# The down product of a hybrid encoder block: row blocks added onto banks, columns finished in two halves, T2 and T4 on VectorE

## Chip, cores and metric

The kernel runs on one core of a Trainium2 chip. The metric is device time in microseconds (us) of one execution; the figures below are the median, lowest and highest of three runs, and one more execution was taken with the hardware profiler.

## What is computed

One layer of a bidirectional hybrid encoder on x of shape (1, 512, 1024) in float32. The change concerns the last part only, the down product of the gated convolution MLP with the norm and residual behind it.

```python
x = x + _rmsnorm(merged @ w_out, g_post_mix)          # x1
h2 = _rmsnorm(x, g_pre_ffn)
...
hid = h @ w_up                                         # 1024 -> 2 x 2816
hid = conv(hid, conv_w) + conv_b
a, b = jnp.split(hid, 2, axis=-1)
return (jax.nn.gelu(a) * b) @ w_down                   # (512, 2816) @ (2816, 1024)
...
x = x + _rmsnorm(mlp, g_post_ffn)
```

## The kernel before

Every float32 product is done as three matmuls on a high and a low part (`split`: ACT copies the high part, L75; VectorE subtracts the low part, L82). Weights lie in HBM as blocks of 128 x 1024 (`wall`), and `units` lists in which order and in which form they are wanted. `w_get` hands out the next unit and prepares those that follow, as many as five of size two with the one handed out: an SP transfer into a raw tile (four of these), then the forms, then `split` into the slots `w4` (nine of these). All engines run their own queue in order; the order within a queue is set by a scheduler that simulates the program, so it is not always that of the source.

The 22 row blocks of `w_down` (128 rows each) are used in two ways. The first 18 make 9 pairs (`DP`), and each pair is a 2 x 2 block product done by a scheme with seven products instead of eight (M1 to M7, `UNITS`). A pair needs two units per half of the output columns: form `q` (the raw quarters, 768 columns) and form `t` (T1 to T4, 1024 columns, made in `w_down`: T1 and T3 by VectorE in one instruction, L167, T2 and T4 by GpSimd, L171 and L172). The left-hand forms come from `down_forms`, of which seven are made while the up product runs (`EAGER`) and two in the first half of the down product. `products` runs nine pairs x seven products x six matmuls of 256 columns (L974) into seven PSUM banks, once for the output columns 0 to 511 and once for 512 to 1023; `combine` (L980 to L994) then forms the four quarters `c11`, `c12`, `c21`, `c22` of each half from the seven banks.

The last 4 row blocks (`RES_DOWN`) are kept aside: their weights are split into tiles that stay (`held`), the left-hand side by `two_parts` during the second half (`some`). When both halves are done, the last loop goes over the 4 row tiles of 128 rows (`NT`) and both column halves: 12 matmuls of 512 columns, two additions of the `combine` results (L1025), the square with its row sum on ACT (L802), the multiplication by `gpf` (L1029); then `row_scale` on GpSimd (L810), the final multiply and add (L1033) and the transfer out (L1036), issued by SP and ACT in turn.

Of the kernel before, what the change touches and what calls it, by code (L numbers as in the profile page):

```python
# [12 lines left out]
AF = mybir.ActivationFunctionType  # L13
ALU = mybir.AluOpType

P = 128
D = 1024
# [12 lines left out]
NBLK = 74  # L30
WARM = 18
RES_OUT = 6
RES_DOWN = 4
DOWN0 = NW - NF
DP = (NF - RES_DOWN) // 2
# [8 lines left out]
def tile_block(ctx: ExitStack, tc, xT, x, wall, par, cs, decay, wsp, bsp, gpost, gffn, out):  # L44
# [45 lines left out]
    while i < NW:  # L90
        pair = [(f, i) for f in ("B11", "B21", "T1", "T2", "T3", "T4", "B22")]
        if U0 <= i < GATE0:
            units += pair
            i += 2
        elif GATE0 <= i < GATE1:
            units += pair[:4] + [("blk", i + 2)] + pair[4:] + [("blk", i + 3)]
            i += 4
        elif DOWN0 <= i < DOWN0 + 2 * DP:
            units += [("q", i), ("t", i)]
            i += 1  # L100
        else:
            units.append(("blk", i))
            i += 1
# [5 lines left out]
    def slot(n, at=0, w=1024):  # L109
        return sb.tile([P, 1088], F32R, tag="w4", bufs=9, name=nm(n))[:, at : at + w]  # L110

    def w_block(i):
        raw = raw_tile() if i else raw0
        resident = RES0 <= i < RES1 or i >= NW - RES_DOWN
# [9 lines left out]
        else:  # L124
            hi, lo = slot("wh"), slot("wl")
# [32 lines left out]
    def w_down(form, i):  # L158
# [5 lines left out]
        else:  # L164
# [6 lines left out]
            nc.gpsimd.tensor_tensor(out=raw[:, 512:768], in0=raw[:, :256], in1=b[:, 256:512], op=ALU.add)  # L171
            nc.gpsimd.tensor_tensor(out=raw[:, 768:], in0=raw[:, 512:768], in1=b[:, 512:768], op=ALU.add)  # L172
# [120 lines left out]
    wst = const("wst", [P, S])  # L293
# [69 lines left out]
    rbc = const("rbc", [P, S])  # L363
# [593 lines left out]
    M1, M2, M3, M5, M6, M7, M4 = range(7)  # L957

    def products(between):
        m = [None] * 7  # L960
        for j in range(DP):
            between(j)
            for n, (unit, at, act) in enumerate(UNITS):
                if n in (0, 3):
                    wh, wl = w_get()
                if j == 0:
                    m[n] = ps()
                f = slice(at * 256, (at + 1) * 256)
                ah, al = dforms[j][act]
                for t in range(2):  # L970
                    c = slice(t * P, (t + 1) * P)
                    o = m[n][:, t * 256 : (t + 1) * 256]
                    for i, (a_, w_) in enumerate(((ah, wh), (ah, wl), (al, wh))):
                        nc.tensor.matmul(  # L974
                            o, a_[:, c], w_[:, f], start=j == t == i == 0, stop=j == DP - 1 and i == 2,
                            skip_group_check=True,
                        )
        return m

    def combine(m):  # L980

        e1, e5, e3, uu = tmp("e1"), tmp("e5"), tmp("e3"), tmp("uu")
        c11, c12, c21, c22 = (blk(n="c") for _ in range(4))
        copy(e1, m[M1])
        v.tensor_add(c11, m[M2], e1)  # L985
        copy(e3, m[M3])
        copy(e5, m[M5])
        v.tensor_add(uu, m[M6], e1)
        v.tensor_add(e1, m[M7], uu)  # L989
        v.tensor_add(c21, m[M4], e1)  # L990
        v.tensor_sub(c22, e5, e1)
        v.tensor_add(e3, e3, e5)  # L992
        v.tensor_sub(c12, e3, uu)
        return [[c11, c12], [c21, c22]]  # L994

    late = list(range(EAGER, DP))
    some = []

    def first_pass(j):
        if late and j % 2:  # L1000
            down_forms(late.pop(0))

    def second_pass(j):
        if j % 2 and len(some) < RES_DOWN:
            some.append(two_parts(gp[2 * DP + len(some)]))

    cc = [combine(products(first_pass))]
    m = products(second_pass)
    held = [w_get() for _ in range(RES_DOWN)]
    cc.append(combine(m))  # L1010
    gpf = bcast(gffn, "gpf")
    for t in range(NT):
        q = small("q", 2, 4)
        xt = halves("x1")
        z = []
        for n in range(2):
            nc.sync.dma_start(xt[n], x1[t][n])
            o = ps()
            c = slice(t * P, (t + 1) * P)
            for i, ((ah, al), (wh, wl)) in enumerate(zip(some, held)):  # L1020
                mm3(o, ah[:, c], al[:, c], wh[n], wl[n], i == 0, i == RES_DOWN - 1)
            z.append(tmp("z"))
            for i in range(2):
                f = slice(i * 256, (i + 1) * 256)
                v.tensor_add(z[n][:, f], o[:, f], cc[n][t // 2][i][:, (t % 2) * 256 : (t % 2 + 1) * 256])  # L1025
            mean_square(q, n, z[n])
            if n:
                sc = row_scale(q)
            v.tensor_mul(z[n], z[n], gpf[n])  # L1029
        for i, (a, b) in enumerate(((0, 512), (512, 768), (768, 1024)) if t == NT - 1 else ((0, 512), (512, 1024))):  # L1030
            f = slice(a % S, a % S + b - a)
            zt = z[a // S][:, f]
            v.scalar_tensor_tensor(  # L1033
                out=zt, in0=zt, scalar=sc, in1=xt[a // S][:, f], op0=ALU.mult, op1=ALU.add
            )
            (nc.sync, nc.scalar)[i % 2].dma_start(out[t, :, a:b], zt)  # L1036
# [34 lines left out]
def _quads(a):  # L1071

    b = a.reshape(DP, 2, P, 2, 2, 256)
    return np.stack([
        np.concatenate([b[:, 0, :, n, 0], b[:, 1, :, n, 1], b[:, 1, :, n, 0], b[:, 0, :, n, 1]], -1) for n in range(2)
    ]).reshape(2 * DP, P, 1024)
# [65 lines left out]
```

## Time and profile before

| | |
|---|---|
| median of three runs | 853.29 us (850.13 to 853.82) |
| the profiled execution | 849.69 us |
| its span, first to last instruction | 847.5 us |
| PE busy (TensorE products) | 828.0 us, 98% |
| VectorE (DVE) busy | 612.7 us, 72% |
| ScalarE (ACT) busy | 401.9 us, 47% |
| GpSimd (POOL) busy | 126.1 us, 15% |

The profile names engines PE (products), PEld (weight loads), DVE, ACT, POOL and SP (which issues transfers). A row of a timeline gives the start, the duration, the engine and line, what is written from what, and in brackets how long the engine stood idle before and for what. A PE that counts as busy is not one at its peak, since products are pipelined.

### The profile page before, as it was taken

The page shows a single profiled execution, that of the slowest core. Times are in us where ns is not written, and L with a number is a line of the kernel's source. Part 1 is how long each engine was busy: PE and PEld are TensorE (multiplying, and loading weights), DVE is VectorE, ACT ScalarE, POOL GpSimd, SP SyncE. Part 2 cuts the span into 40 slices and gives each one's busy share as a digit, 9 for nine tenths or more (in the row PEclk, how much of TensorE's full clock was granted, in tenths as well). Part 3 has the DMA queues.
Part 4 walks back from the last instruction along what each step waited for, and adds up shares of the span by engine and source line. Part 5 has one row for each costly group of instructions (what it writes and reads, how often), then busy time and mean ns, then how long its engine had stood idle before and what let it go on. Part 6 is the DMA issues. An engine that isn't in the chain of part 4 may idle for free. (4 is left out here: it accounts for less than half of the span.)

```text
span 847.5 us, 12239 instructions
## 1 busy us (share of the span) xinstructions
PE 828.0 (98%) x4768; PEld 727.7 (86%) x4768; DVE 612.7 (72%) x966; ACT 401.9 (47%) x647; POOL 126.1 (15%) x123
## 2 busy tenths in 40 slices
PE   8999999999999999999999999999999999998993
PEld 6888888888999999999988998888888888998982
DVE  5598888877996677777755677666666555877675
ACT  6645446545664544344544564444444333443332
POOL 0010000111221111122212200000000001463601
PEclk9999999999999999999999999999999999999997
DMA  8732222213233233323556133333222221223352
GB/s 276 250 113 100 77 73 75 74 51 100 87 101 100 100 100 100 100 100 100 175 178 244 50 100 100 100 100 99 100 93 90 94 73 50 75 101 100 102 203 94
DMA packets 29242, 93.18 MB, mean 110 GB/s; under 512 B 3392, under 2 KB 4032, under 8 KB 29184
## 3 DMA queue, kind: packets, MB, share of 16 engines
q1 hardware_dynamic: 26928, 86.85, 30.6%
q0 software_dynamic: 1392, 4.46, 1.6%
q10 hardware_dynamic: 864, 1.09, 0.4%
q8 instruction: 37, 0.61, 0.3%
q14 instruction: 21, 0.17, 0.1%
HBM read 88.19 MB, written 4.19 MB: 109 GB/s over the span
## 5 line engine op out<-in xcount | busy, mean ns | idle before, releaser
L82 DVE TENSOR_TENSOR wl<-raw,wh 128x1024 fp32r<-128x1024 f32 (+1 forms) x113 | 128.5, 1147 | 105.3 <-PE ps L199 63.8
L200 PE MATMUL ps<-h2h,wl 128*128 128x512 f32 (+1 forms) x384 | 142.3, 371 | 0.0
L199 PE MATMUL ps<-h2l,wh 128*128 128x512 f32 (+1 forms) x384 | 142.2, 371 | 0.0
L198 PE MATMUL ps<-h2h,wh 128*128 128x512 f32 (+1 forms) x384 | 142.2, 372 | 0.0
L75 ACT ACTIVATE wh<-raw 128x1024 fp32r<-128x1024 f32 (+2 forms) x115 | 110.2, 970 | 43.8 <-DMA raw<-wall 24.6
L75 ACT ACTIVATE wf<-raw 128x512 fp32r<-128x512 f32 x84 | 50.8, 627 | 73.6 <-issue 30.2
L198 PEld LDWEIGHTS ps<-h2h,wh 128*128 128x128 f32 x384 | 72.1, 188 | 12.8 <-ACT h2h L858 0.3
L199 PEld LDWEIGHTS ps<-h2l,wh 128*128 128x128 f32 x384 | 72.2, 188 | 12.6
L200 PEld LDWEIGHTS ps<-h2h,wl 128*128 128x128 f32 x384 | 72.2, 188 | 12.3
L82 DVE TENSOR_TENSOR wf<-raw,wf 128x512 fp32r<-128x512 f32 x84 | 65.6, 797 | 20.0 <-ACT wf L75 19.6
L901 ACT ACTIVATE cv<-ps,part 128x512 f32<-128x512 f32 x44 | 34.4, 781 | 87.9 <-PE ps L200 87.9
L459 PE MATMUL ps<-wh,xh 128*128 128x512 f32 x192 | 75.0, 391 | 0.0
L460 PE MATMUL ps<-wl,xh 128*128 128x512 f32 x192 | 74.9, 390 | 0.0
L461 PE MATMUL ps<-wh,xl 128*128 128x512 f32 x192 | 74.8, 390 | 0.0
L646 PE MATMUL ps<-sh,wf 128*128 128x256 f32 x384 | 72.6, 280 | 0.0
L171 POOL TENSOR_TENSOR raw<-raw,raw 128x256 f32<-128x256 f32 x18 | 25.2, 1401 | 271.1 <-DVE raw L167 253.8
L974 PE MATMUL ps<-dh,fh 128*128 128x256 f32 x216 | 60.6, 281 | 1.3 <-DVE c L985 1.3
L974 PE MATMUL ps<-dl,fh 128*128 128x256 f32 x216 | 60.5, 280 | 1.1 <-DVE dl L82 1.1
L646 PEld LDWEIGHTS ps<-sh,wf 128*128 128x128 f32 x384 | 60.8, 188 | 0.5 <-ACT u L75 0.2
L974 PE MATMUL ps<-dh,fl 128*128 128x256 f32 x216 | 60.4, 280 | 0.0
L646 PE MATMUL ps<-xh,wf 128*128 128x256 f32 x288 | 54.6, 281 | 0.0
L646 PE MATMUL ps<-sl,wf 128*128 128x256 f32 x192 | 53.6, 279 | 0.0
(276 smaller groups left out, 1873.9 us busy)
## 6 DMA issues: line engine op xcount, KB each, us to landing
raw<-wall SPq DMA_DIRECT2D x145, 512.0 KB, 3.3
x<-x SPq DMA_DIRECT2D x24, 256.0 KB, 5.7
xT<-xT SPq DMA_DIRECT2D x8, 256.0 KB, 5.5
x<-x POOLq DMA_DIRECT2D x8, 256.0 KB, 2.3
xT<-xT POOLq DMA_DIRECT2D x4, 256.0 KB, 3.8
out<-z SPq DMA_DIRECT2D x4, 256.0 KB, 2.0
out<-z ACTq DMA_DIRECT2D x3, 256.0 KB, 2.1
cs<-cs SPq DMA_DIRECT2D x2, 256.0 KB, 5.0
```

What stands on the lines that cost most here:

```text
L75: nc.scalar.activation(out=o, in_=i, func=AF.Copy)
L82: nc.vector.tensor_sub(lo, src, as32(hi))
L171: nc.gpsimd.tensor_tensor(out=raw[:, 512:768], in0=raw[:, :256], in1=b[:, 256:512], op=ALU.add)
L198: nc.tensor.matmul(o, ah, bh, start=start, stop=False)
L199: nc.tensor.matmul(o, ah, bl, start=False, stop=False)
L200: nc.tensor.matmul(o, al, bh, start=False, stop=stop)
L459: nc.tensor.matmul(acc[t], xh[k][:, c], wh[:, f], start=k == 0, stop=False)
L460: nc.tensor.matmul(acc[t], xh[k][:, c], wl[:, f], start=False, stop=False)
L461: nc.tensor.matmul(acc[t], xl[k][:, c], wh[:, f], start=False, stop=k == KD - 1)
L646: nc.tensor.matmul(o, w_[:, c], a_, start=first and k == n == 0, stop=k == 3 and n == 2, skip_group_check=True,)
L901: nc.scalar.activation(out=c, in_=o, func=AF.Identity, scale=col(CW + 3 * m + 1), bias=col(CB + m))
L974: nc.tensor.matmul(o, a_[:, c], w_[:, f], start=j == t == i == 0, stop=j == DP - 1 and i == 2, skip_group_check=True,)
```

## The change

- The 4 last row blocks are no longer a product of their own. A new function `add_whole` adds them straight onto banks of the pair products: for the row tiles 0 and 1 onto M2 and M3 (from which the quarters `c11` and `c12` follow), for 2 and 3 onto M4 (`c21`) and onto an eighth bank M8, which is added to `c22`. Its matmuls have 256 columns. A weight block now holds two row blocks for one half of the columns.
- In the first half of the columns these blocks come after the pairs 3 and 5; in the second half after all nine pairs.
- The sums of the banks run inside the last pair, right after the product that closes each bank (`steps`). In the second half the last sum is taken for each row tile in the last loop.
- The first 512 columns are finished mid-way: their share of the square sum (in two pieces, added to the other half's later) and the product with `gpf` are made after the pairs 2 to 5 of the second half (`first_share`). The last loop has only the other 512 columns.
- `two_parts` of the four left-hand blocks moves into pairs 0 to 3 of the first half.
- T2 and T4 of form `t` are made by VectorE instead of GpSimd.
- `rbc` and `wst` lie in the common pool `blk`, which has 76 tiles instead of 74. The resident tiles of the four blocks are gone; their units use the slots `w4`.

The core of the diff (removed lines of the last part and the host's reordering of `w_down` are left out):

```diff
@@ -27,12 +27,12 @@
 NW = 146
 U0, GATE0, GATE1 = 32, 40, 72
 LOOK = 4
-NBLK = 74
+NBLK = 76
 WARM = 18
 RES_OUT = 6
-RES_DOWN = 4
 DOWN0 = NW - NF
-DP = (NF - RES_DOWN) // 2
+DP = 9
+WHOLE = NF - 2 * DP
 EAGER = 7
 PRE, FFNG, LNG, LNB = 0, 8, 16, 24
@@ -95,9 +95,13 @@
         elif GATE0 <= i < GATE1:
             units += pair[:4] + [("blk", i + 2)] + pair[4:] + [("blk", i + 3)]
             i += 4
-        elif DOWN0 <= i < DOWN0 + 2 * DP:
-            units += [("q", i), ("t", i)]
-            i += 1
+        elif i == DOWN0:
+            for _ in range(2):
+                pairs = [[("q", i + j), ("t", i + j)] for j in range(DP)]
+                whole = [[("blk", i + DP)], [("blk", i + DP + 1)]]
+                for u in pairs[:4] + whole[:1] + pairs[4:6] + whole[1:] + pairs[6:] if i == DOWN0 else pairs + whole:
+                    units += u
+                i += DP + WHOLE // 2
         else:
             units.append(("blk", i))
             i += 1
@@ -111,7 +115,7 @@
     def w_block(i):
         raw = raw_tile() if i else raw0
-        resident = RES0 <= i < RES1 or i >= NW - RES_DOWN
+        resident = RES0 <= i < RES1
         if i > 0:
             nc.sync.dma_start(raw, wall[i])
         if resident:
@@ -122,7 +126,8 @@
                 hi.append(h_)
                 lo.append(l_)
         else:
-            hi, lo = slot("wh"), slot("wl")
+            at = 48 if i >= DOWN0 else 0
+            hi, lo = slot("wh", at), slot("wl", at)
             if i == 0:
                 pieces = [slice(0, P), slice(P, S), slice(S, 2 * S)]
                 for f in pieces:
@@ -168,8 +173,8 @@
                 out=raw[:, :512].rearrange(two, n=2), in0=b[:, :512].rearrange(two, n=2),
                 in1=b[:, None, 768:].to_broadcast([P, 2, 256]), op=ALU.add,
             )
-            nc.gpsimd.tensor_tensor(out=raw[:, 512:768], in0=raw[:, :256], in1=b[:, 256:512], op=ALU.add)
-            nc.gpsimd.tensor_tensor(out=raw[:, 768:], in0=raw[:, 512:768], in1=b[:, 512:768], op=ALU.add)
+            nc.vector.tensor_add(raw[:, 512:768], raw[:, :256], b[:, 256:512])
+            nc.vector.tensor_add(raw[:, 768:], raw[:, 512:768], b[:, 512:768])
         w = 768 if form == "q" else 1024
         hi, lo = slot("dh", 48, w), slot("dl", 48, w)
         split(hi, lo, raw)
@@ -290,7 +295,7 @@
     make_identity(nc, ident)
     ones = const("ones", [P, P])
     nc.gpsimd.memset(ones, 1.0)
-    wst = const("wst", [P, S])
+    wst = blk(n="wst")
     nhalf = const("nhalf", [P, 16])
     nc.gpsimd.memset(nhalf, -0.5)
@@ -360,7 +365,7 @@
             start=True,
             stop=True,
         )
-    rbc = const("rbc", [P, S])
+    rbc = blk(n="rbc")
     copy(rbc, rb)
     copy(wst[:, 0:1], rbc[:, 0:1])
     cosr, sinr = halves("cs")
@@ -954,86 +959,132 @@
     UNITS = (("q", 0, "A11"), ("q", 2, "A12"), ("q", 1, "S4"), ("t", 0, "S1"), ("t", 2, "S2"), ("t", 1, "S3"), ("t", 3, "A22"))
...
+    M1, M2, M3, M5, M6, M7, M4, M8 = range(8)
+    whole = []
+    def products(m, j, steps={}):
+        for n, (unit, at, act) in enumerate(UNITS):
+            if n in (0, 3):
+                wh, wl = w_get()
+            if j == 0:
+                m[n] = ps()
+            f = slice(at * 256, (at + 1) * 256)
+            ah, al = dforms[j][act]
+            for t in range(2):
+                c = slice(t * P, (t + 1) * P)
+                o = m[n][:, t * 256 : (t + 1) * 256]
+                for i, (a_, w_) in enumerate(((ah, wh), (ah, wl), (al, wh))):
+                    nc.tensor.matmul(
+                        o, a_[:, c], w_[:, f], start=j == t == i == 0,
+                        stop=j == DP - 1 and i == 2 and n not in (M2, M3, M4), skip_group_check=True,
+                    )
+            steps.get(n, lambda: None)()
+    def add_whole(m, t, g, w, last=False):
+        wh, wl = w
+        c = slice(t * P, (t + 1) * P)
+        for n, b in enumerate(((M2, M3), (M4, M8))[t // 2]):
+            o = m[b][:, (t % 2) * 256 : (t % 2 + 1) * 256]
+            for k in range(2):
+                f = slice(k * S + n * 256, k * S + (n + 1) * 256)
+                ah, al = whole[2 * g + k]
+                for i, (a_, w_) in enumerate(((ah, wh), (ah, wl), (al, wh))):
+                    nc.tensor.matmul(
+                        o, a_[:, c], w_[:, f], start=b == M8 and t == 2 and g == k == i == 0,
+                        stop=last and k == 1 and i == 2, skip_group_check=True,
+                    )
+    m = {}
+    m[M8] = ps()
+    late = list(range(EAGER, DP))
+    c11, c12, c21, c22 = c4 = [blk(n="c") for _ in range(4)]
+    e1, e3, uu, yy = tmp("e1"), tmp("e3"), tmp("uu"), tmp("yy")
+    def after6():
         v.tensor_add(uu, m[M6], e1)
+        v.tensor_sub(c12, m[M5], uu)
+        v.tensor_add(c12, c12, e3)
+    def after7():
         v.tensor_add(e1, m[M7], uu)
...
+        v.tensor_sub(yy, m[M5], e1)
+        v.tensor_add(c22, c22, yy)
+    steps = {
+        M1: lambda: copy(e1, m[M1]),
+        M2: lambda: v.tensor_add(c11, m[M2], e1),
+        M3: lambda: copy(e3, m[M3]),
+        M6: after6, M7: after7,
+        M4: lambda: v.tensor_add(c21, m[M4], e1),
+    }
+    for j in range(DP):
+        if j < WHOLE:
+            whole.append(two_parts(gp[2 * DP + j]))
+        if j % 2 and late:
             down_forms(late.pop(0))
...
+        products(m, j, steps if j == DP - 1 else {})
+        if j in (3, 5):
+            w = w_get()
+            for t in range(NT):
+                add_whole(m, t, j // 2 - 1, w, j == 5)
+            if j == 5:
+                copy(c22, m[M8])
     gpf = bcast(gffn, "gpf")
+    qn = [small("q", 4, 4) for _ in range(NT)]
+    zg = []
+    def first_share(t):
+        zg.append(blk(n="zg"))
+        for i in range(2):
+            src = c4[2 * (t // 2) + i][:, (t % 2) * 256 : (t % 2 + 1) * 256]
+            j = tmp("junk")
+            nc.scalar.activation(out=j[:, :256], in_=src, func=AF.Square, scale=D ** -0.5, accum_out=qn[t][:, 2 + i : 3 + i])
+            v.tensor_mul(zg[t][:, i * 256 : (i + 1) * 256], src, gpf[0][:, i * 256 : (i + 1) * 256])
+        v.tensor_add(qn[t][:, 0:1], qn[t][:, 2:3], qn[t][:, 3:4])
+    m = {}
+    e1, uu, xx, yy = tmp("e1"), tmp("uu"), tmp("xx"), tmp("yy")
+    def after6():
+        v.tensor_add(uu, m[M6], e1)
+        v.tensor_sub(xx, m[M5], uu)
+    def after7():
+        v.tensor_add(uu, m[M7], uu)
+        v.tensor_sub(yy, m[M5], uu)
+    steps = {M1: lambda: copy(e1, m[M1]), M6: after6, M7: after7}
+    for j in range(DP):
+        products(m, j, steps if j == DP - 1 else {})
+        if 1 < j < 2 + NT:
+            first_share(j - 2)
+    ww = [w_get(), w_get()]
+    m[M8] = ps()
     for t in range(NT):
...
         xt = halves("x1")
...
         for n in range(2):
             nc.sync.dma_start(xt[n], x1[t][n])
...
+        for g in range(2):
+            add_whole(m, t, g, ww[g], g == 1)
+        z, zs_ = tmp("z"), tmp("zs")
+        for i, (b, e) in enumerate((((M2, e1), (M3, xx)), ((M4, uu), (M8, yy)))[t // 2]):
+            f = slice((t % 2) * 256, (t % 2 + 1) * 256)
+            v.tensor_add(z[:, i * 256 : (i + 1) * 256], m[b][:, f], e[:, f])
+        mean_square(qn[t], 1, z)
+        v.tensor_mul(zs_, z, gpf[1])
+        sc = row_scale(qn[t])
+        zt = (zg[t], zs_)
         for i, (a, b) in enumerate(((0, 512), (512, 768), (768, 1024)) if t == NT - 1 else ((0, 512), (512, 1024))):
             f = slice(a % S, a % S + b - a)
...
+            o = zt[a // S][:, f]
             v.scalar_tensor_tensor(
...
+                out=o, in0=o, scalar=sc, in1=xt[a // S][:, f], op0=ALU.mult, op1=ALU.add
             )
...
+            (nc.sync, nc.scalar)[i % 2].dma_start(out[t, :, a:b], o)
 def _parts(a, n, w):
```

More of the change, by code (lines that the diff above doesn't have):

```diff
@@ L956, in tile_block @@
     UNITS = (("q", 0, "A11"), ("q", 2, "A12"), ("q", 1, "S4"), ("t", 0, "S1"), ("t", 2, "S2"), ("t", 1, "S3"), ("t", 3, "A22"))
[L957 to L978, printed above, removed]
@@ L994, in combine @@
[L994 to L1000, printed above, removed]
-            down_forms(late.pop(0))
[L1003 to L1010, printed above, removed]
-    gpf = bcast(gffn, "gpf")
+        v.tensor_sub(yy, m[M5], e1)
@@ L1071, in _quads, with _down @@
 def _quads(a):
[L1073 to L1076, printed above, removed]
+    b = a.reshape(DP, 2, P, 2, 256)
+    return np.concatenate([b[:, 0, :, 0], b[:, 1, :, 1], b[:, 1, :, 0], b[:, 0, :, 1]], -1)
+def _down(a):
+    r = 2 * DP * P
+    return np.concatenate([
+        p for n in range(2) for c in [a[:, n * S : (n + 1) * S]]
+        for p in (_quads(c[:r]), c[r:].reshape(WHOLE // 2, 2, P, S).transpose(0, 2, 1, 3).reshape(-1, P, 1024))
+    ])
 def _cols(a):
```

31 lines of the change are left out of this document (1 added, 30 removed).

## The prediction

> **What bounds the kernel now.** I read the page's first lines, then the stretch that the change rewrites by windows, then PE's waits, the chain of waits and the timeline of each engine there.
>
> ```profile
> span 847.5 us, 12239 instructions
> ```
>
> ```profile
> core 0: us, PE busy (x) PEld busy (x) DVE busy (x) ACT busy (x) POOL busy (x), PEclk, DMA share, GB/s
> 719.10:764.90 45.80, 45.80 (x390) 45.80 (x389) 35.52 (x44) 22.08 (x29) 23.69 (x16) 1.00 0.27 93
> 764.90:812.30 47.40, 43.56 (x370) 42.70 (x369) 33.36 (x39) 18.77 (x26) 20.47 (x16) 1.00 0.40 126
> 812.30:834.30 22.00, 21.93 (x98) 17.82 (x96) 16.95 (x34) 6.42 (x16) 1.88 (x2) 1.00 0.36 137
> 834.30:847.50 13.20, 0.00 (x0) 0.00 (x0) 6.75 (x15) 2.17 (x6) 1.86 (x2) 0.58 0.22 80
> ```
>
> ```profile
> PE ps L974 <- DVE dl L82: 2.6, 3, 1.1
> PE ps L974 <- DVE c L985: 1.3, 1, 1.3
> ```
>
> The four windows are my cut of the down product: the pairs of the first 512 columns, those of the second (with the start of the row blocks' last preparation), the four row blocks, and what comes after PE's last product. PE never pauses in the first window, loses 47.40 - 43.56 = 3.8 us in the second, works through the third, and has nothing to do in the last 13.2. So the stage can give at most the 3.8 us of pauses and part of the 13.2; the products themselves stay. The two rows of waits name the pauses: 1.3 us for a PSUM bank that `combine` had not yet read (L985), 2.6 us in three waits for the low half of a weight (L82).
>
> **Products.** Before, 756 matmuls of 256 columns and 96 of 512; after, `add_whole` makes the 96 into 192 of 256, half of them after pairs 3 and 5 of the first half, half at the end. The count of columns is the same. PE runs the 256-wide ones at two paces. The first two rows below are the start of a pair's M2 and of the next pair's M1, 36 matmuls apart; the next two are the same places in the second half.
>
> ```profile
> 759.38 0.28 PE L974 MATMUL ps<-dh,fh 128*128 128x256 f32 x1
> ...
> 763.62 0.28 PE L974 MATMUL ps<-dh,fa 128*128 128x256 f32 x1
> ...
> 775.58 0.28 PE L974 MATMUL ps<-dh,fh 128*128 128x256 f32 x1
> ...
> 779.66 0.28 PE L974 MATMUL ps<-dh,fa 128*128 128x256 f32 x1
> ```
>
> 4.24 / 36 = 0.1178 us against 4.08 / 36 = 0.1133, with a granted clock of 1.00 in both windows. The row blocks' 512-wide ones follow each other at 22.0 / 96 = 0.229, twice 0.1146. All 948 cost 107.4 us at the fast pace and 111.4 at the first window's 45.80 / 390 = 0.1174. Which pace holds seems to be decided anew after a pause; I can't say which it will be and take the middle, 0.1155, so 109.5 us.
>
> The row says that halving a matmul costs between nothing and 192 x 0.0041 = 0.8 us here. The Trainium skill, page "TensorE: Matmul & The Clock Gate", section "Back-to-back issue gap", speaks mildly against the change: it gives 262 cycles for 256 columns and 518 for 512, so two halves cost 6 cycles more than one whole. By its figures, as an estimate, the 96 halved products would add 0.24 us, which lies within the row's two ends.
>
> **Weights: the loop that takes the place of GpSimd.** The chain of waits over the second half shows one turn per pair:
>
> ```profile
> 790.00 3.42 DMA raw<-wall
> ...
> 793.52 0.06 DVE raw L167
> ...
> 794.13 0.96 DVE dl L82
> ...
> 795.15 4.84 DMA raw<-wall
> ```
>
> A weight lands, VectorE adds T1 and T3 (L167), then subtracts the low half of the pair before (L82, 768 wide); that frees a raw tile, and only then does SP start the next transfer. VectorE works in order, so L167, which waits for the transfer, stands ahead of the subtraction that allows the next one. A turn is 795.15 - 790.00 = 5.15 us, against 42 x 0.1174 = 4.93 for a pair on PE. The loader is slightly slower than PE, and where a transfer takes 4.84 instead of 3.42 PE pauses. T2 and T4 are off this loop now, since GpSimd forms them:
>
> ```profile
> L171 POOL TENSOR_TENSOR raw<-raw,raw 128x256 f32<-128x256 f32 x15 | 23.0, 1534 | 46.9 <-DVE raw L167 29.5 <-ACT dh L75 11.4 <-ACT fh L75 4.5
> L172 POOL TENSOR_TENSOR raw<-raw,raw 128x256 f32<-128x256 f32 x15 | 20.1, 1338 | 1.2
> ```
>
> ```profile
> 730.08 5.02 POOL L171 TENSOR_TENSOR raw<-raw,raw 128x256 f32<-128x256 f32 x1 [6.17 <-ACT dh L75]
> 735.18 0.73 POOL L172 TENSOR_TENSOR raw<-raw,raw 128x256 f32<-128x256 f32 x1
> ```
>
> ```profile
> 724.39 0.41 DVE L82 TENSOR_TENSOR fa<-gp,fa 128x256 fp32r<-128x256 f32 x1
> 724.73 0.41 DVE L930 TENSOR_TENSOR fs<-gp,gp 128x256 f32<-128x256 f32 x1
> ```
>
> On GpSimd they take 1.53 + 1.34 = 2.9 us a pair, once 5.02 for an addition that took 0.73 the next time. On VectorE 256-wide steps follow each other at 0.34 (724.39 to 724.73), so 0.68 a pair. The form T thus comes 2.2 us earlier, but VectorE pays 0.68, and if both additions follow L167 at once, which is what their order in the code suggests, the turn grows to about 5.8 us.
>
> Load is not the limit. First half: VectorE's 35.5 us plus 18 x 0.34 = 6.1 plus the four `two_parts` (512 wide, no more than two 256-wide steps, 0.82) come to 45 of 45.8 + 10.9 = 56.7 us. So the four and the two late `down_forms` in pairs 0 to 3 are hidden; without the row blocks behind pair 3 they would not all be. Latency is the limit: at 5.8 a turn against 42 x 0.1155 = 4.85 a pair, nine pairs lose 8.5 us. In the first half the two row blocks pay for it, each 5.5 us of PE time for one unit to load. In the second half only the lead does: five units may be loaded or in work, two pairs, of which about one, 5 us, can be used up. That leaves 3.5 us of pauses (ends: 0, if the scheduler puts the additions elsewhere, and 8.5), about what there is now.
>
> **After PE's last product.** The end of the third row tile and the last one, from the timeline:
>
> ```profile
> 836.60 1.42 DVE L1033 SCALAR_TENSOR_TENSOR z<-z,qr,x 128x512 f32<-128x512 f32 x2 [0.44 <-POOL qr L810]
> ...
> 837.93 1.08 DVE L1025 TENSOR_TENSOR z<-ps,c 128x256 f32<-128x256 f32 x3
> 838.04 0.34 ACTq L1036 DMA_DIRECT2D out<-z  x1
> ...
> 840.08 0.42 DVE L1025 TENSOR_TENSOR z<-ps,c 128x256 f32<-128x256 f32 x1
> ...
> 841.34 0.16 DVE L807 SCALAR_TENSOR_TENSOR qs<-q 128x1 f32<-128x1 f32 x1 [0.85 <-ACT junk L802]
> 841.42 0.69 DVE L1029 TENSOR_TENSOR z<-z,gpf 128x512 f32<-128x512 f32 x1
> 841.58 0.93 POOL L810 TENSOR_TENSOR qr<-qs,nhalf 128x1 f32<-128x1 f32 x1 [5.02 <-DVE qs L807]
> 842.54 1.54 DVE L1033 SCALAR_TENSOR_TENSOR z<-z,qr,x 128x512 f32<-128x512 f32 x3 [0.44 <-POOL qr L810]
> ```
>
> PE is done by 834.3 (the last window shows none of it), but the last tile's sums begin at 837.93: VectorE stands behind the tile before. Its last step ends at 842.54 + 1.54 = 844.1, 9.8 us behind PE, and 3.4 us of output follow. After the change a tile has one half row left: two 256-wide adds, one square, one multiplication, the scale and the two final steps. From the last add (840.08) to the end it took 4.0 us; with one more add ahead, 0.34, a tile's chain is 4.3. VectorE's own part is 0.68 + 0.69 + 0.16 + 1.42 = 2.95. PE gives a tile every 24 x 0.1155 = 2.8, the first 8.3 us before its end. If tile after tile runs in order, as now, VectorE ends 4 x 4.3 - 8.3 = 8.9 us behind PE; if the next tile's adds fill the waits, 3 x 2.95 + 4.3 - 8.3 = 4.9. ACT's queue decides too: the output that ACT issues (838.04) stands ahead of the next tile's square and waits for the last step. Products now come faster than the chain, which favours filling; I take the middle, 6.9, so 2.9 us gained. The first 512 columns' share (squares, multiplications) lies beside pairs 2 to 5, 4 x (2 x 0.34 + 0.16) = 3.4 us of VectorE, inside that window's 14 us of idle VectorE. The sums L985 to L993 end within the last pair and M4 instead of after PE.
>
> **The bank wait.** The 1.3 us go: `products` now calls the sums as soon as each bank closes (`steps`), and M1 of the second half gets the bank of M8, which is copied to `c22` already after pair 5. What is late next is the bank of M5, which `yy` reads only after M7; M6 of the second half may need it. Between lie M7, M4 and four products of the second half, 36 x 0.1155 = 4.2 us after M6 closes; VectorE needs five 512-wide steps up to `yy`, 5 x 0.69 = 3.5. It just fits; if a wait of L167 for its transfer falls into it, it costs up to the old 1.3.
>
> Waits that the change adds: at the end of each half VectorE's sums wait for their bank to close while the next weights' forms queue behind them, at most one product, 0.7 us, each; the lead covers it. The first share's multiplications wait for `gpf`, whose two transfers on GpSimd's queue are issued at the change of halves, two pairs (9.7 us) ahead of the first use; that queue holds no additions any more. The `x1` loads stay on SP's queue behind the last weights. All three at nothing; without the cover each stands in the pauses' upper end. The two tiles moved to the common pool (`rbc`, `wst`) and its two more buffers keep the room as it was: nothing.
>
> **Sum.** 719.1 + 109.5 (products) + 3.5 (pauses) + 6.9 + 3.4 = 842.4 us of span, 5.1 less than 847.5. The profiled execution took 849.69 us, 2.2 more than its span and 0.4% under the median of the runs shown, 853.29; I take the 5.1 off the median: 848.2 us.
>
> **Rivals.** *The loop binds in both halves* (slower): T2 and T4 ahead of the subtraction, and the lead never builds up, because pairs 0 to 3 carry `down_forms` and `two_parts`. Then 18 x 0.95 = 17.1 us less about 1 at each row block, so 15 of pauses instead of 3.5: 859.7. For it: L167 stands ahead of the subtraction today. Against it: no pause in the first window though VectorE is busy there from the start. It cancels the gain at 8.6 us of pauses, and is slower by over 0.5% from 12.9. Chance 0.14.
> *The gain goes into order* (no change): slow pace throughout (111.4), 6 us of pauses, VectorE strictly tile by tile (8.9): 848.8 of span, 854.6. It needs only that the scheduler keeps today's order. Chance 0.25.
> *All fits* (large gain): 0.5 us of pauses because the T form no longer waits for GpSimd, and a filled tail of 4.9: 837.4 of span, 843.2. Chance 0.18.
> *The change doesn't do what it says*: M5's bank is held and the middle wait stays at 1.3; that moves the forecast to 849.5 and is inside it.
>
> **How the numbers follow.** The forecast has 0.43. About 0.5%, 4.3 us, is what a measurement of this kernel can tell from no change. Forecast and large gain make faster 0.61, the second rival same 0.25, the first slower 0.14. All good ends at once give 840.6 and all bad ones (111.4, 8.5, 8.9) 857.1; I leave out the outermost and the slower rival: 842 to 856.5.
>
> **What would show it.** Right: no wait for a bank at the change of halves; GpSimd with only the scales left; VectorE's last step 5 to 9 us behind PE; pauses only in the late pairs of the second half, each for `dl`, with a turn near 5.8 between transfers. Wrong: pauses of more than 8.6 us on L82, above all in the first half, or VectorE further than 9 us behind PE.

## The result and the profile after

The changed kernel takes 841.86 us (median of four runs, 841.50 to 844.99) against 853.56 (850.13 to 855.06) for the kernel before, run beside it: a ratio of 0.9877, with a 95% interval of 0.9839 to 0.9915. So it is faster, by 1.2%. The forecast was 848.2; the median lies 6.3 us below it and 0.1 us below the low end of the stated range. A second comparison of the same two kernels (e5_new_again, below) gave 0.9893, interval 0.9868 to 0.9918.

The first lines of the page of after, and the down product in windows of its own (the pairs up to the second row block; the rest of the pairs; the row blocks of the last loop; what follows PE's last product):

```profile
span 839.8 us, 12386 instructions
PE 827.2 (98%) x4864; PEld 731.3 (87%) x4864; DVE 615.1 (73%) x996; ACT 401.5 (48%) x649; POOL 76.0 (9%) x87
```

```profile
core 0: us, PE busy (x) PEld busy (x) DVE busy (x) ACT busy (x) POOL busy (x), PEclk, DMA share, GB/s
719.30:760.40 41.10, 41.10 (x350) 41.09 (x349) 34.25 (x55) 19.84 (x27) 0.59 (x1) 1.00 0.34 109
760.40:818.40 58.00, 58.00 (x506) 57.86 (x505) 45.43 (x72) 26.37 (x42) 0.54 (x1) 1.00 0.41 133
818.40:831.40 13.00, 11.89 (x98) 11.26 (x96) 9.54 (x21) 2.17 (x6) 1.66 (x3) 1.00 0.22 83
831.40:839.80 8.40, 0.00 (x0) 0.00 (x0) 4.11 (x8) 0.72 (x2) 0.55 (x1) 0.71 0.33 125
```

PE never pauses in the pairs of either half: 41.10 of 41.10 and 58.00 of 58.00. Before, the second half lost 3.8 us. The stretch without PE at the end is 8.4 us long instead of 13.2. GpSimd, 23.69 and 20.47 us busy in the two halves before, has one step in each of the first two windows, the issue of a transfer of `gpf`, and the scale steps in the last two. All of PE's waits from 715 us on are in one line of the list of waits:

```profile
PE ps L993 <- DVE z L1076: 1.0, 2, 0.5
```

Because the down product does not begin at the same time in every execution (718.2 to 726.2 us over the traces; they differ mostly in the program's first 50 us, far ahead of the change, where PE waits 0.3 to 3.7 us for the first weights), I compare it from its own first product. "Lag" is the time from the end of PE's last product to the end of VectorE's last step, "drain" the time from there to the span's end; "stage" is the sum. The last column names PE's waits in the stage.

| kernel | PE | lag | drain | stage | PE's waits (us) |
|---|---|---|---|---|---|
| before | 115.1 | 9.9 | 3.4 | 128.4 | low halves 2.6, bank 1.3 |
| before, once more (e11_old_again) | 115.2 | 9.7 | 3.4 | 128.3 | low halves 2.4, bank 1.2 |
| after | 112.0 | 5.2 | 3.4 | 120.5 | last loop 1.0 |
| after, once more (e5_new_again) | 112.8 | 5.1 | 3.4 | 121.3 | last loop 1.1, banks 0.5 |

The stage is 7.9 us shorter, 3.2 in PE's part and 4.7 in the lag. The two profiled executions differ by about the same (849.69 and 841.63 us), the medians by 11.7.

### The profile page after: what moved, and what is told of

Read it like the earlier page. It is cut to its first block, busy times and chain, and to the rows that moved or that the text cites. A ratio compares the mean times of both kernels' runs of the same rounds, so it can differ in the third digit from the quotient of the medians.

```text
span 839.8 us, 12386 instructions
## 1 busy us (share of the span) xinstructions
PE 827.2 (98%) x4864; PEld 731.3 (87%) x4864; DVE 615.1 (73%) x996; ACT 401.5 (48%) x649; POOL 76.0 (9%) x87
## 4 chain that ended last, share of the span: by engine, by line
PE 96%; DVE 1%; DMA 1%; issue 1%; ACT 0%; POOL 0%; DVEq 0%; SPq 0%; POOLq 0%; ACTq 0%
PE ps L204 16%; PE ps L203 16%; PE ps L205 16%; PE ps L651 14%; PE ps L977 10%; PE ps L465 5%; PE ps L464 5%; PE ps L466 5%; PE ps L798 2%; PE ps L796 2%; PE ps L797 2%; PE ps L993 2%; PE ps L721 1%; DMA raw<-wall 1%; PE ps L264 1%
## 5 line engine op out<-in xcount | busy, mean ns | idle before, releaser
L82 DVE TENSOR_TENSOR wl<-raw,wh 128x1024 fp32r<-128x1024 f32 (+1 forms) x109 | 128.2, 1184 | 100.0 <-PE ps L204 63.7
L75 ACT ACTIVATE wf<-raw 128x512 fp32r<-128x512 f32 x84 | 50.8, 627 | 73.5 <-issue 30.2
L82 DVE TENSOR_TENSOR wf<-raw,wf 128x512 fp32r<-128x512 f32 x84 | 65.8, 799 | 19.9 <-ACT wf L75 19.6
L82 DVE TENSOR_TENSOR dl<-raw,dh 128x768 fp32r<-128x768 f32 (+1 forms) x36 | 39.2, 1091 | 18.7 <-PE ps L204 7.9
```

The lines of the kernel that those rows point to most:

```text
L75: nc.scalar.activation(out=o, in_=i, func=AF.Copy)
L82: nc.vector.tensor_sub(lo, src, as32(hi))
```

## The experiments

The theory after the first comparison of the traces: before, T2 and T4 on GpSimd kept ACT waiting, ACT's copies of later weights stood behind, and the weights came late; VectorE's faster additions cure that. The rivals: the row blocks in the first half give the loader slack (and the additions don't matter), or the shorter last loop alone brings the gain. Each ratio is to the kernel before, run on the same chip, over five rounds, with its 95% interval.

### e1_new_gpsimd_t and e2_old_vector_t: the two parts apart

e1 is after with T2 and T4 back on GpSimd; e2 is before with them on VectorE.

```diff
-            nc.vector.tensor_add(raw[:, 512:768], raw[:, :256], b[:, 256:512])
-            nc.vector.tensor_add(raw[:, 768:], raw[:, 512:768], b[:, 512:768])
+            nc.gpsimd.tensor_tensor(out=raw[:, 512:768], in0=raw[:, :256], in1=b[:, 256:512], op=ALU.add)
+            nc.gpsimd.tensor_tensor(out=raw[:, 768:], in0=raw[:, 512:768], in1=b[:, 512:768], op=ALU.add)
```

> The changed kernel with T2 and T4 back on GpSimd, nothing else. Theory GpSimd (its slow additions hold the T form and the ACT queue behind it, and that made the pauses before): 2 to 4 us of pauses of PE on L82 come back in the pairs, span about 842 to 844. Theory queue (the pauses came from VectorE standing at L172 for a transfer while only four raw tiles exist; the row blocks in the middle cure it): pauses stay under 0.5 us and the span stays within 1 us of 839.8.

> The kernel before with T2 and T4 on VectorE, nothing else. Theory GpSimd: the 2.6 us of waits on L82 go, only the 1.3 for the bank stays, and the span falls by about 2.5 us from 847.5. Theory queue: turns of 5.1 us between transfers remain and so do 2 to 4 us of pauses; span within 1.5 us of 847.5. My blind prediction's term (turns of 5.8 us) would give pauses of 6 us or more and a longer span.

Measured: e1 844.69 us, ratio 0.9896 (0.9876 to 0.9916), stage 120.9 (PE 112.2, lag 5.0, drain 3.7). e2 844.14 us, ratio 0.9889 (0.9870 to 0.9908), stage 120.5 (PE 111.0, lag 6.1, drain 3.4). Each part of the change alone brings as much as the whole, as far as these intervals and traces can tell; together they bring no more. The theory of the queue foresaw e1, but neither foresaw so much of e2. The windows of e2:

```profile
720.40:764.90 44.50, 44.50 (x379) 44.46 (x379) 40.78 (x65) 22.82 (x30) 0.00 (x0) 1.00 0.29 98
764.90:809.30 44.40, 44.40 (x379) 44.40 (x379) 35.85 (x55) 21.18 (x29) 1.13 (x2) 1.00 0.49 158
809.30:831.40 22.10, 22.10 (x99) 18.02 (x98) 15.73 (x33) 4.34 (x12) 2.29 (x3) 1.00 0.22 83
831.40:840.90 9.50, 0.01 (x1) 0.00 (x0) 4.36 (x11) 1.45 (x4) 0.86 (x1) 0.77 0.29 110
```

No pause is left, and the tail is short although its code is that of before. Why, the timeline of VectorE shows: first before, then e2, the first sum of the second half's banks (L985), and the first sum of the last loop (L1025).

```profile
814.62 0.68 DVE L985 TENSOR_TENSOR c<-ps,e 128x512 f32<-128x512 f32 x1
...
819.39 0.75 DVE L1025 TENSOR_TENSOR z<-ps,c 128x256 f32<-128x256 f32 x2
```

```profile
807.72 0.68 DVE L985 TENSOR_TENSOR c<-ps,e 128x512 f32<-128x512 f32 x1
...
812.49 0.75 DVE L1025 TENSOR_TENSOR z<-ps,c 128x256 f32<-128x256 f32 x2
...
835.96 1.54 DVE L1033 SCALAR_TENSOR_TENSOR z<-z,qr,x 128x512 f32<-128x512 f32 x3 [0.44 <-POOL qr L810]
```

Before, the row blocks of PE began at 812.3 and L985 ran at 814.62, 2.3 us after; in e2 they began at 809.5 and L985 ran at 807.72, 1.8 us ahead. From the first L1025 to the end of the last L1033 VectorE needs the same in both: 844.1 - 819.4 = 24.7 us and 837.5 - 812.5 = 25.0. So late weights cost twice before: 3.8 us of pauses, and a tail that started late. The chain of waits of before shows how the second cost arises:

```profile
808.09 4.57 DMA raw<-wall
812.74 1.15 ACT wh L75 x2
813.89 1.47 ACT e L75 x3
```

The last weights land at 812.7; ACT copies their high parts first, and only then the banks (`e`) that the sums start from.

Where the weights lost time shows in ACT's waits in the pairs, first before, then after, then e1:

```profile
ACT dh L75 <- POOL raw L172: 35.3, 12, 6.5
```

```profile
ACT dh L75 <- PE ps L977: 24.0, 17, 2.0
ACT dh L75 <- DVE raw L177: 7.8, 3, 3.0
```

```profile
ACT dh L75 <- POOL raw L177: 22.0, 7, 5.8
```

ACT stood 35.3 us, up to 6.5 at a time, for T4 of GpSimd, and everything else in its queue stood behind that. In after it stands mostly for PE, that is for a slot whose weights PE still reads: the loader is ahead (before, these waits came to 1.5 us). Waiting for GpSimd is not a price by itself, though. In e1 ACT still stands 22.0 us for T4, up to 5.8 at a time, and PE's only wait in the pairs is 0.3 us for a bank. With GpSimd's additions e2 also takes away the late T form and the slower subtractions of VectorE (last section); which of these counts was not taken apart.

### e12_new_gpsimd_blocks_end: does the slack do it in e1?

e1, and the row blocks of the first half behind its nine pairs, with the sums of that half behind them.

```diff
-                for u in pairs[:4] + whole[:1] + pairs[4:6] + whole[1:] + pairs[6:] if i == DOWN0 else pairs + whole:
+                for u in pairs + whole:
...
-        if j in (3, 5):
...
+    w2 = [w_get(), w_get()]
+    for t in range(NT):
+        for g in range(2):
+            add_whole(m, t, g, w2[g], g == 1)
```

> The changed kernel with T2 and T4 on GpSimd, as in e1_new_gpsimd_t, and with the row blocks of the first half behind its nine pairs instead of behind pairs 3 and 5 (the sums of M2, M3, M4 and M8 follow them). Theory slack (row blocks in the midst of the pairs give the loader time, and that is what spared e1 the pauses): 2 to 5 us of pauses on L82 or on the sums come back in the pairs of the first half, stretch 123 to 126 instead of 120.9. Rival (early two_parts and the sums at each bank's end spared them): stretch 120.5 to 122.

Measured: 844.29 us, ratio 0.9915 (0.9885 to 0.9945), stage 121.9 (PE 112.9, lag 5.0, drain 4.0).

```profile
PE ps L993 <- DVE z L1078: 1.0, 2, 0.6
PE ps L977 <- DVE dl L82: 1.0, 2, 0.6
```

The waits for low halves come back, but only 1.0 us of them. The slack of the two row blocks can so be only part of why e1 does without VectorE's additions; this run also moves the sums of the banks, and the rest wasn't taken apart.

### e4_old_five_raw and e6_old_parts_early: other cures for the old kernel

e4 gives before a fifth raw tile; e6 makes `two_parts` of the last row blocks in the first half, as after does. Both keep T2 and T4 on GpSimd.

```diff
-NBLK = 74
+NBLK = 72
...
-        return sb.tile([P, 1024], F32, tag="raw", bufs=4, name=nm("raw"))
+        return sb.tile([P, 1024], F32, tag="raw", bufs=5, name=nm("raw"))
```

```diff
     def first_pass(j):
+        if j < RES_DOWN:
+            some.append(two_parts(gp[2 * DP + j]))
...
     def second_pass(j):
-        if j % 2 and len(some) < RES_DOWN:
-            some.append(two_parts(gp[2 * DP + len(some)]))
+        pass
```

> The kernel before with five raw tiles instead of four, and 72 instead of 74 tiles in the common pool to make room. Theory queue: a transfer no longer waits for the subtraction behind L167, PE's pauses in the pairs fall from 3.9 us to under 1, span about 844 (unless the smaller pool costs something ahead of the down product, which the start of the first pair, 719.1, shows). Theory GpSimd: pauses stay at 2 to 4 us.

> The kernel before with the four two_parts moved from the second half into pairs 0 to 3 of the first, as the change does, and nothing else; T2 and T4 stay on GpSimd. Theory ACT queue (the copies of two_parts stand on ACT behind the copy of form T, which waits for GpSimd, and VectorE's subtractions wait for those copies; that is what made the weights late in the second half): the wait at the fourth pair goes, at most 1.5 us of pauses stay, the stretch falls from 128.4 to 122 to 125. Rival (the turn between transfers alone makes them late): pauses of 3 to 4 us stay, stretch 127 to 129.

Measured: e4 849.93 us, ratio 0.9953 (0.9936 to 0.9970), stage 124.4; e6 849.02 us, ratio 0.9962 (0.9944 to 0.9979), stage 126.9. PE's waits in e4, then in e6:

```profile
PE ps L974 <- DVE dl L82: 3.0, 2, 1.9
```

```profile
PE ps L974 <- DVE c L985: 4.4, 1, 4.4
PE ps L974 <- DVE dl L82: 0.6, 1, 0.6
```

With a fifth raw tile the bank wait goes and the lag falls to 6.8, half the gain, but the low halves stay late: the ring of raw tiles is not the cause alone. With `two_parts` out of the second half the low halves come nearly in time (0.6 us), although ACT still stands 30.2 us for GpSimd, and the bank wait grows to 4.4. So the waits that e6 was to cure went, and the gain that was expected of it (122 to 125) did not come. VectorE's timeline in e6 shows why:

```profile
768.26 0.69 DVE L167 TENSOR_TENSOR raw<-raw 128x512 f32<-128x512 f32 x1 [3.56 <-DMA raw<-wall]
768.87 0.68 DVE L985 TENSOR_TENSOR c<-ps,e 128x512 f32<-128x512 f32 x1
```

The sum that frees the bank stands behind an L167 that waits 3.56 us for its transfer. This is the same in-order queue that makes the turn, at another place: a wait for a transfer ahead of a step that somebody needs. The long wait costs a second time: in the 3.6 us behind it the granted clock was 0.53, and 17 products took 0.21 us each instead of 0.11, 1.7 us more.

### e3_new_share_late: what finishing the first columns mid-way is worth

After, with `first_share` taken out of the pairs and put into the last loop. A small step on each quarter, which adds zero times a result of the second half, keeps the scheduler from taking the share ahead again.

```diff
-        if 1 < j < 2 + NT:
-            first_share(j - 2)
+    for c in c4:
+        v.scalar_tensor_tensor(
+            out=c[:, 0:1], in0=yy[:, 0:1], scalar=0.0, in1=c[:, 0:1], op0=ALU.mult, op1=ALU.add
+        )
...
     for t in range(NT):
+        first_share(t)
```

> The changed kernel with the first 512 columns' squares and multiplications made behind the last pair instead of beside pairs 2 to 5 (four one-column steps tie them to the last sum). Theory: the tail is VectorE's work per row tile, so 4 x (2 x 0.34 + 0.16) + 4 x 0.16 = 4 us of VectorE more after the last pair, VectorE's last step 8 to 9 us behind PE instead of 5.2, span 842.5 to 844. Rival (the tail is a chain of waits and the added steps fill them): span within 1 us of 839.8.

Measured: 848.63 us, ratio 0.9943 (0.9923 to 0.9963), against 0.9896 for e1 in the same rounds and 0.9893 for e5 in others; stage 122.9. So mid-way finishing is worth about 2 us in the stage (122.9 - 121.3 = 1.6 and 122.9 - 120.5 = 2.4), the small tying steps included. The place is another than I thought: the lag is shorter (3.75), and PE waits instead:

```profile
PE ps L993 <- DVE z L1079: 3.4, 1, 3.4
```

VectorE, late with the shares, is late with the sum that reads the first half of a bank, and PE's next product writes to the other half of it. Behind this wait, too, the granted clock was 0.50 (835.6 to 838.5 us), and 16 gaps between products were 0.213 us instead of 0.113: 1.6 us of what e3 loses is this slowing.

### e7_new_order and e9_new_tail: the last loop

In e7 the row tiles of the last loop come in the order 0, 2, 1, 3, so that two tiles that share banks don't follow each other. e9 does that, takes `z` and `zs` from the common pool, and writes the final steps of a tile behind the sums of the next.

```diff
-    for t in range(NT):
+    for t in (0, 2, 1, 3):
```

```diff
+    for t in ORDER:
...
-        z, zs_ = tmp("z"), tmp("zs")
+        z, zs_ = blk(n="z"), blk(n="zs")
...
         v.tensor_mul(zs_, z, gpf[1])
+        if ready:
+            finish(*ready)
+        ready = (t, (zg[t], zs_), xts[t], row_scale(qn[t]))
+    finish(*ready)
```

> The changed kernel with the row tiles of the last loop in the order 0, 2, 1, 3, so that two tiles that follow each other use different banks. Theory (PE's two waits of 0.5 us in the last loop are for the other half of a bank that VectorE still reads): both waits go, PE ends 1 us earlier; VectorE's tail is its own work, so the span gains 0 to 1 us. Rival (the waits have another cause): they stay.

> The changed kernel with its last loop rearranged: row tiles in the order 0, 2, 1, 3, the two half-row tiles z and zs in the common pool instead of the six-tile ring (in run e7_new_order a square on ACT waited 5.1 us for an output that still read its tile), and the final multiply-add of a row tile written behind the next tile's sums. Theory (VectorE's tail is the serial chain add, square, scale, multiply-add of each tile, about 3.6 us a tile, and some of it can overlap): PE's two waits go (1.0 us), VectorE's last step 4 to 5 us behind PE, stretch from the first product of the pairs 118 to 119.5 instead of 120.5 to 121.3. Rival (the scheduler puts the steps back in today's order): stretch 120 to 121.

Measured: e7 846.11 us, ratio 0.9912 (0.9885 to 0.9939), stage 123.0 (PE 110.6, lag 9.0); e9 845.53 us, ratio 0.9888 (0.9857 to 0.9919), stage 119.9 (PE 110.1, lag 6.4). In e7 PE's waits for `z` are gone, and the tail is worse; ACT's timeline says where:

```profile
830.91 0.63 ACT L807 ACTIVATE junk<-z 128x512 f32<-128x512 f32 x1 [5.12 <-DMA out<-zs]
```

The square waited 5.12 us because its scratch tile, in a ring of six, was still being read by an output transfer. e9 takes that ring out of the way: PE has no wait in the whole stage, and its stage is the shortest of all. Its ratio can't be told from that of after (0.9877 and 0.9893), so it isn't shown to be better; the lag of 4 to 5 us that was expected did not come.

### e8_new_pause and e10_new_extra: the pace of the products

Apart from the slow products just named, the 256-wide products run at one of two paces in all traces. e8 adds one product near the start of the down product that waits for a copy on ACT; e10 adds the same product without anything to wait for. It goes into a bank that the first row block starts anew.

```diff
+            if j == n == 0 and whole_open:
+                d = blk(F32R, "pause")
+                copy(d[:, :P], m[M1][:, :P])
+                nc.tensor.matmul(m[M8][:, :P], d[:, :P], wh[:, :P], start=True, stop=True, skip_group_check=True)
```

```diff
+            if j == n == 0 and extra:
+                nc.tensor.matmul(m[M8][:, :P], ah[:, :P], wh[:, :P], start=True, stop=True, skip_group_check=True)
```

> The changed kernel with one deliberate pause of PE behind the first product of the first pair: ACT copies 128 columns of that bank, and an extra 128-column product with the copy (into the bank M8, which is opened later) has to wait for it, about 1 us. In the traces the 256-wide products run at 0.118 or 0.113 us apart and change over only where PE has just paused. Theory pace (a pause resets the pace to the faster one): from there on 0.1133, about 0.0043 x 500 = 2 us less for the pairs, 1 us net. Rival (the pace has another cause): 0.118 in the first half as before, about 1 us more.

> The changed kernel with one extra product of 128 columns behind the first product of the first pair, into the bank M8, which is opened later; nothing waits. In e8_new_pause, with a wait of 1.6 us at this place, all 256-wide products ran at 0.113 us. Theory pause (the wait set the pace): without it 0.118 in the first half, stretch 120.5 to 121.5. Rival (the odd product set the pace): 0.113 from there on, about 2 us less for the products, stretch 118.5 to 120.5, as far as no sum is then waited for.

Measured: e8 845.14 us, ratio 0.9910 (0.9878 to 0.9941), stage 122.5; e10 844.72 us, ratio 0.9887 (0.9852 to 0.9921), stage 122.4. The start of M2 in the second pair and of M1 in the third, 36 products apart, in e8 and in e10:

```profile
726.82 0.28 PE L977 MATMUL ps<-dh,fh 128*128 128x256 f32 x1
...
730.90 0.28 PE L977 MATMUL ps<-dh,fa 128*128 128x256 f32 x1
```

```profile
726.28 0.28 PE L977 MATMUL ps<-dh,fh 128*128 128x256 f32 x1
...
730.52 0.28 PE L977 MATMUL ps<-dh,fa 128*128 128x256 f32 x1
```

4.08 / 36 = 0.1133 us after a wait, 4.24 / 36 = 0.1178 without one, and each kernel keeps its pace from there through both halves (after itself turns from the slow to the fast one near 780 us, at the change of halves). So the wait changed the pace here, and the extra product did not, by one trace of each. A wait does not always bring the faster pace: before, 36 products from 775.58 on took 4.08 us, and 36 from 783.39 on, just behind a wait of 1.07 us, took 4.24. It didn't pay: e8 spent 1.6 us on the wait itself, and the faster PE then met a bank that VectorE had not yet read:

```profile
PE ps L977 <- DVE e L1017: 1.7, 1, 1.7
PE ps L985 <- ACT pause L75: 1.6, 1, 1.6
```

### e5_new_again and e11_old_again: the two kernels once more

Unchanged kernels, for the size of the effect and for the spread between traces.

> The changed kernel once more, unchanged, beside the other three. In the earlier traces the stretch from the first product of the down pairs to the end was 128.4 us before, 120.5 with the whole change, 120.9 with all of it but GpSimd forming T2 and T4, and 120.5 with T2 and T4 on VectorE in the old kernel and nothing else. Theory either (one cure for the late weights suffices, the parts don't add up): 120.5 +- 1 again and a ratio to the kernel before of about 0.988, the same as those two. Rival (the parts add up, the two earlier timings were held back by the state of that chip): ratio under 0.985.

> The kernel before once more, unchanged, for a second trace. Its first trace began the pairs at 719.1 us; the traces of the other kernels began them between 718.2 and 726.2, according to how long PE had waited for the very first weights. Theory: the stretch from the first product of the pairs to the end is 127.5 to 129.5 again, with 3 to 5 us of pauses of PE on L82 and L985. Rival (the pauses of the first trace were those of one execution): stretch under 126.

Measured: e5 843.87 us, ratio 0.9893 (0.9868 to 0.9918); e11, one execution, 850.59 us. Their stages stand in the first table: two traces of one kernel agree within 0.8 us there.

## Why the prediction was right, and where its size was wrong

The direction and the places were right, the size was short: 5.1 us of span forecast, 7.7 measured. The mechanism was right only in part: the prediction took T2 and T4 on VectorE for a step that lengthens the turn and keeps the pauses, and e2 shows that this step alone brings as much as the whole change. Term by term:

| term of the sum | forecast | measured in after |
|---|---|---|
| start of the stage | 719.1 | 719.3 |
| 948 products | 109.5 (107.4 to 111.4) | 112.0 - 1.0 = 111.0 |
| pauses | 3.5 (0 to 8.5) | 1.0, none of them in the pairs |
| tail lag | 6.9 (4.9 to 8.9) | 5.2 |
| drain | 3.4 | 3.4 |

**The turn: the step that failed.** I put T2 and T4 right behind L167, ahead of the subtraction, and got a turn of 5.8 us. VectorE's timeline of after, one turn (L172 is now the line of T1 and T3, L176 and L177 are T2 and T4):

```profile
767.06 0.69 DVE L172 TENSOR_TENSOR raw<-raw 128x512 f32<-128x512 f32 x1 [0.43 <-DMA raw<-wall]
767.67 0.95 DVE L82 TENSOR_TENSOR dl<-raw,dh 128x768 fp32r<-128x768 f32 x1
768.54 0.42 DVE L176 TENSOR_TENSOR raw<-raw,raw 128x256 f32<-128x256 f32 x1
768.99 0.43 DVE L177 TENSOR_TENSOR raw<-raw,raw 128x256 f32<-128x256 f32 x1
770.34 1.23 DVE L82 TENSOR_TENSOR dl<-raw,dh 128x1024 fp32r<-128x1024 f32 x1 [0.93 <-PE ps L977]
771.83 0.69 DVE L172 TENSOR_TENSOR raw<-raw 128x512 f32<-128x512 f32 x1 [0.26 <-DMA raw<-wall]
```

Here the scheduler kept the subtraction directly behind L172 and set the two additions after it, so they lie off the loop of the raw tile: the turn is 771.83 - 767.06 = 4.8 us, no longer than a pair on PE. The order is not the same in every turn. L172 waited for its transfer in four (at 754.12, 767.06, 771.83 and 802.89); the subtraction comes ahead of both additions in three of them and behind one in the first, and the turns that end there took 3.4, 5.4, 4.8 and 5.3 us. None reached 5.8, and the 24.0 us that ACT stood for PE's slots show that the loop did not set the pace. That was the end at zero that I had named ("if the scheduler puts the additions elsewhere") and not taken. I had also seen only the loop of transfers and not ACT's queue, where the old placing cost 35.3 us of waits; e2, which takes the additions off GpSimd and changes nothing else, brings as much as the whole change. The forecast's "T form comes 2.2 us earlier" was counted at nothing, though the additions now take 0.43 us each; the rival "All fits" (843.2) rested on it, and was nearer.

**The slower rival**, the loop that binds in both halves, is out: no pause on L82 at all.

**The tail.** The lag is near the end that I called filled. The next tile's first sum goes into the wait for the scale; its second still stands behind the final steps:

```profile
830.56 0.42 DVE L1076 TENSOR_TENSOR z<-ps,uu 128x256 f32<-128x256 f32 x1
831.37 0.75 DVE L1084 SCALAR_TENSOR_TENSOR zg<-zg,qr,x 128x512 f32<-128x512 f32 x1 [0.39 <-POOL qr L815]
832.04 0.75 DVE L1084 SCALAR_TENSOR_TENSOR zs<-zs,qr,x 128x512 f32<-128x512 f32 x1
832.70 0.42 DVE L1076 TENSOR_TENSOR z<-ps,yy 128x256 f32<-128x256 f32 x1
...
835.57 0.87 DVE L1084 SCALAR_TENSOR_TENSOR zs<-zs,qr,x 128x256 f32<-128x256 f32 x2
```

But part of the long tail of before came from the late weights (e2: 6.1 with the old code), which my reckoning of the tail took for a property of its order.

**The bank wait** at the change of halves went, as forecast, and no other came there in the profiled execution; in e5 0.5 us did, on the reads of two banks. A wait I did not foresee stands in the last loop, 0.5 us twice:

```profile
827.50 0.38 PE L993 MATMUL ps<-wh,fh 128*128 128x256 f32 x1 [0.49 <-DVE z L1076]
...
829.63 0.39 PE L993 MATMUL ps<-wh,fh 128*128 128x256 f32 x1 [0.49 <-DVE z L1076]
```

Row tiles that follow each other share their two banks, so a product into one half waits for the sum that reads the other; e7 and e9, with the tiles in another order, have no such wait.

**Products** cost 111.0 / 948 = 0.1171 each, near the slow pace; halving the row blocks' matmuls lies hidden in that spread. (Before, the 512-wide ones follow each other at 0.2267, twice the fast pace; the forecast's 0.229 took in the edges of its window.)

**What stays open.** The stage explains 7.9 us, the medians differ by 11.7 in the first comparison and by 8.1 in the second. Both traces of before (849.69 and 850.59 us) are among its quicker executions; the 50 others of the experiments took 849.20 to 857.68. The traces show one place where executions differ, the start of the program: in the window from 10 to 20 us the granted clock was 0.68 to 0.87 in the four traces that begin the stage at 722.0 us or later (e3, e4, e5, e7), and 0.93 to 1.00 in the ten that begin it by 720.5. In both traces of before it was 1.00. The mean clock of a whole execution was 0.994 and 0.995 in these two and 0.988 to 0.993 in 45 of the 50 others, so many of those may have begun late; no trace shows it, nor why the clock was lower.

## What to carry to other kernels

When an engine in the middle of a chain of copies waits on a slow helper, look at the whole queue behind it and at the slack there: here ACT waited 35 us for two small additions, the weights came late, and that cost pauses and then, a second time, a late tail; with slack in the order of the weights (e1), 22 us of the same waits cost nothing. Several parts of a change can cure the same lateness; then each alone brings the gain, they don't add up, and only the parts run apart show which of them is needed. Where a step is added to an in-order queue that a scheduler fills, forecast both places, ahead of and behind the step that frees the buffer, and don't take the source order for the queue's.

## What the runs showed of the hardware

Two paces. Products of 256 columns ran at 0.1133 or 0.1178 us with a granted clock of 1.00 in both, kept the pace over hundreds of products, and behind one wait of 1.6 us it was the faster (e8 against e10), behind one of 1.07 us in before the slower. Over 948 products the difference is 4 us. Why there are two stays open. The Trainium skill, page "TensorE: Matmul & The Clock Gate", section "Back-to-back issue gap", gives a single figure for 256 columns, 262 cycles as the gap of an isolated product; the runs show two.

Behind a long wait of PE the clock was lower. Behind waits of 4.4 us (e6) and 3.4 us (e3) the granted clock was 0.53 and 0.50 over the next 17 products or so, which cost 1.7 and 1.6 us on top of the wait; behind a wait of 1.9 us (e4, 815.2 to 818.0 us) it was 1.00.

GpSimd's additions slow VectorE's. The grouped rows of the 1024-wide subtraction and of the two additions in after:

```profile
L82 DVE TENSOR_TENSOR dl<-raw,dh 128x1024 fp32r<-128x1024 f32 x17 | 20.8, 1226 | 12.4 <-PE ps L977 4.3 <-PE ps L993 4.0 <-PE ps L204 2.9
L176 DVE TENSOR_TENSOR raw<-raw,raw 128x256 f32<-128x256 f32 x15 | 6.4, 425 | 0.2
L177 DVE TENSOR_TENSOR raw<-raw,raw 128x256 f32<-128x256 f32 x15 | 6.4, 426 | 0.2
```

The subtraction takes 1226 ns here, 1426 before and 1329 in e1, in the same group, and 1221 in e2, which differs from before only in the engine of the additions; the additions take 0.43 us on VectorE against 1.34 to 1.53 on GpSimd. The Trainium skill, page "SBUF — State Buffer", section "Who interferes with whom", says that a VectorE instruction with two inputs in SBUF contends with a GpSimd instruction that reads SBUF; these rows agree. Seventeen subtractions at 0.2 us are 3.4 us of VectorE that the prediction gave away.
